# Seven normalised token tiles of the residual are copied by DMA into F32R tiles and transposed as F32R, and so is branch B's value tile, in a feed-forward and attention layer

## The chip, the cores and the metric

One core of one Trainium2 chip runs the whole kernel. The metric is the device time of one launch in microseconds, the median of repeated runs. A run here scatters by some tenths of a microsecond, and a difference of 0.2% is 3.8 us.

## What is computed

One layer over 1024 tokens of width 1024, all in float32:

```python
h = x + 0.5 * swiglu(rms_norm(x, ffn1_norm), ffn1_w_gate, ffn1_w_up, ffn1_w_down)   # D_FF = 2816
u = rms_norm(h, mix_norm)
qa, ka, va, qb, kb, vb, ga, gb = split(u @ w_in)                                    # 4352 columns
ya = neighbourhood_attention_2d(qa, ka, va, na_rpb)
yb = windowed_gqa_sink(rope(qb), rope(kb), vb, sink_logit)
h = h + (sigmoid(ga) * (ya @ w_branch_a) + sigmoid(gb) * (yb @ w_branch_b)) @ w_out
h = h + 0.5 * swiglu(rms_norm(h, ffn2_norm), ffn2_w_gate, ffn2_w_up, ffn2_w_down)
y = rms_norm(h, final_norm)
```

## The kernel before

The stages follow each other: the first feed-forward block, the projection to the 4352 columns, the two attentions with the merge, the second feed-forward block, and the last norm. Every large product is done by Strassen's seven products of half-size blocks, and every factor is split into a high part rounded to F32R (the reduced float32 type of TensorE) and the rest, so `mm3` issues three F32R matmuls of 128x512 for each block: high by high on L149, high by low on L153, low by high on L155. ACT makes the high part (L95, or L327 for weights) and DVE the low part (L98, L334). A tile named `g` or `d` is a PSUM bank, four of each; `fa` and `fx` are the residual and work rows, `ar` the right operands, `ws` the split left operands, `raw` and `ahead` loaded weights, `xs` two buffers of 128x1024.

Between a product that leaves the residual h in token rows and a product that needs the normalised rows turned (features on partitions) stands a `transition` (L167). There are two: the first between the down product of the first block and the projection (L1261), the second between the product with `w_out` and the second feed-forward block (L1815). The change works in these two. Eight tiles of 128 tokens pass through, and for tile t the steps are:

- `pre(t)`: from tile 4 on the tail of the finishing product (matmuls of TensorE into `g` or `d`, and the addition into the residual by DVE on L640), and a write of the row to DRAM from the SP queue.
- `normed` (L119): ACT squares the row into an `xs` buffer and sums it into the small tile `st` (L127), POOL adds epsilon and takes the power -1/2 (L130, L131), DVE scales the row into the same `xs` buffer (L133).
- `turned` (L137): eight transposes of 128x128 by TensorE on L142, with the `xs` block as weights and `ident` as the moving operand, into two `d` banks.
- `to_strassen` (L198): the operands of the next product. For tiles 0 to 3 they are split by L95 and L98 and copied by L211 and L212; from tile 4 on the Strassen sums stand in between (DVE L216, L218, L221, L222, then L95 and L98), and in the first transition a copy of a half row (L225).
- `post(t-1)`: from tile 4 on ten steps of the next product's matmuls, which are to cover the steps of the next tile.

The program issues tile t+1's `normed` ahead of tile t's `turned`, so the two `xs` buffers alternate: one is normed while the other is transposed. The buffer for the square of tile t+2 comes free when TensorE has transposed tile t. In the second transition the two tiles 4 and 5 are computed further ahead (`ahead` 3).

The order on every engine is fixed when the program is built: a scheduler places the instructions from the program order and its own estimates of durations, and what is pinned (`pin`) keeps its place. At run time each engine takes its own list in order, and an instruction that waits holds all behind it. POOL's list holds the `st` operations, and also the issue of every DMA of `nc.gpsimd` (writes of `hid`, `z_d`, `zs_d`, `g_d`).

In the projection stage `turn_v` (L1158) transposes branch B's values: a row block `vr` in an `xs` buffer, loaded by a DMA of the SP queue, 8 transposes on L1163 into `g` banks, and a split.

Of the kernel before, what the change touches and what calls it, by code (L numbers as in the profile page):

```python
# [9 lines left out]

F32 = mybir.dt.float32
# [4 lines left out]
P = 128  # L16
# [15 lines left out]
def f32v(ap):  # L32
    return ap.bitcast(F32)
# [3 lines left out]
def trunk_kernel(ctx, tc, x, xt, n1, wg1, wu1, wd1, nm, win, rpb, sink, wa, wb, wout,  # L37
# [16 lines left out]
    def nm_(s):  # L54
        uid[0] += 1
        return f"{s}_{uid[0]}"

    ident = const.tile([P, P], F32, name="ident")
    make_identity(nc, ident)
    nhalf4 = const.tile([P, 4], F32, name="nhalf")  # L60
    nc.gpsimd.memset(nhalf4, -0.5)
    nhalf = nhalf4[:, 0:1]
# [23 lines left out]
    def xs4():  # L86
        return main.tile([P, 1024], F32, tag="xs", bufs=2, name=nm_("xs"))
# [32 lines left out]
    def normed(h, gb, xs=None, parts=1):  # L120

        xs = xs4() if xs is None else xs
        w = D // parts
        cols = [slice(i * w, (i + 1) * w) for i in range(parts)]
        st = const.tile([P, 4], F32, tag="st", bufs=4, name=nm_("st"))
        for i, c in enumerate(cols):
            nc.scalar.activation(xs[:, c], h[:, c], AF.Square, scale=D ** -0.5, accum_out=st[:, i:i + 1])  # L127
        if parts == 2:
            nc.gpsimd.tensor_tensor(st[:, 0:1], st[:, 0:1], st[:, 1:2], op=ALU.add)
        nc.gpsimd.tensor_scalar(st[:, 0:1], st[:, 0:1], EPS, None, op0=ALU.add)  # L130
        nc.gpsimd.tensor_tensor(st[:, 2:3], st[:, 0:1], nhalf, op=ALU.pow)  # L131
        for c in cols:
            nc.vector.scalar_tensor_tensor(out=xs[:, c], in0=h[:, c], scalar=st[:, 2:3], in1=gb[:, c],  # L133
                                           op0=ALU.mult, op1=ALU.mult)
        return xs

    def turned(xs):  # L137
        pts = []
        for half in range(2):
            pt = bank("d")  # L140
            for c in range(4):
                nc.tensor.transpose(pt[:, c * P:(c + 1) * P], xs[:, (half * 4 + c) * P:(half * 4 + c + 1) * P], ident)  # L142
            pts.append(pt.rearrange("p (c t) -> p c t", c=4))
        return pts

# [18 lines left out]

        return fx[t] if t < 4 else fa[:, (t - 4) * 1024:(t - 3) * 1024]

    def transition(pre, gain, turn_tile, post, halves=1, ahead=2):  # L167

        h, xs = {}, {}
        n = NTT // halves  # L170
        for base in range(0, NTT, n):
            for t in (base, base + 1):
                h[t] = pre(t)
            xs[base] = normed(h.pop(base), gain)
            yield
            for t in range(base, base + n):
                for k in range(t + 2, t + 1 + ahead) if base and t == base else (t + (ahead if base else 2),):
                    if k < base + n:
                        h[k] = pre(k)
                if t + 1 < base + n:  # L180
                    xs[t + 1] = normed(h.pop(t + 1), gain)
                turn_tile(t, xs.pop(t))
                if t:
                    post(t - 1)
                yield
        post(NTT - 1)
# [6 lines left out]

    kept = []

    def to_strassen(t, xs):

        pa, pb = turned(xs)  # L198
        tt = t % 4
        cols = slice(tt * P, (tt + 1) * P)  # L200

        def put(o, src, eng=None):
            h, l = rhs(o)
            split(h[:, :, cols], l[:, :, cols], src, eng)

        x11 = res(tt)[:, :512].rearrange("p (c t) -> p c t", c=4)
        x21 = res(tt)[:, 512:].rearrange("p (c t) -> p c t", c=4)
        if t < 4:
            put(B11, pa)
            put(B21, pb)  # L210
            nc.scalar.copy(x11, pa)  # L211
            nc.scalar.copy(x21, pb)  # L212
            return
        t1 = res(t)[:, :512].rearrange("p (c t) -> p c t", c=4)
        t2 = res(t)[:, 512:].rearrange("p (c t) -> p c t", c=4)
        nc.vector.tensor_tensor(t1, pa, x11, op=ALU.subtract)  # L216
        put(T1, t1)
        nc.vector.tensor_tensor(t2, pb, t1, op=ALU.subtract)  # L218
        put(T2, t2)
        put(B22, pb)  # L220
        nc.vector.tensor_tensor(x11, t2, x11, op=ALU.subtract)  # L221
        nc.vector.tensor_tensor(x21, x21, t2, op=ALU.subtract)  # L222
        if kept:
            x12 = xs[:, :512] if t == NTT - 1 else main.tile([P, 512], F32, tag="s1", bufs=1, name=nm_("s1"))
            nc.scalar.copy(x12.rearrange("p (c t) -> p c t", c=4), pa)  # L225
            nc.sync.dma_start(kept[0][t - 4], x12)

# [190 lines left out]
    def behind(prods, sooner=()):  # L418

        run, load_ahead = prods[2:4]  # L420

        def post(t):
            if t >= 3:
                drain(run, 10)
            for i, n in zip((1, 2), sooner or (3, 4)):
                if t == n:
                    load_ahead(i)

        return post
# [484 lines left out]
    def keep_busy(n):  # L914

        b = bank("g")
        for i in range(n):
            k = i % 4 * P
            nc.tensor.transpose(b[:, k:k + P], ident, ident)

    def first_stage():
        load, _, _, _, pieces, (multiply, finish), hand_over, load_early = hg
# [39 lines left out]
        def do(op, a):  # L962
# [19 lines left out]
            elif op == "spread":  # L982
                i = int(a[0])
                r[i] = bank("d" if i else "g")
                for k in range(4):
                    nc.tensor.transpose(r[i][:, k * P:(k + 1) * P], st[i][0][:, k:k + 1].to_broadcast([P, P]), ident)
            elif op == "stat":
                t = int(a[0])
                nc.scalar.activation(toks[:, t - 4], toks[:, t - 4], AF.Square, scale=D ** -0.5,
# [162 lines left out]

    def v_b():
        mix["vb"] = [new_fx(k, F32R).rearrange("p (t d) -> p t d", t=NTT) for k in (0, 1)]
        mix["vr"] = xs4()
        pin(nc.sync.dma_start(mix["vr"], z_d[17 * P:18 * P, :]))

    def turn_v():  # L1158
        r = mix["vr"]
        for n in range(2):  # L1160
            pt = bank("g")
            for i in range(4):
                nc.tensor.transpose(pt[:, i * P:(i + 1) * P], r[:, (4 * n + i) * P:(4 * n + i + 1) * P], ident)  # L1163
            pt = pt.rearrange("p (b s d) -> p b s d", s=2, d=HD)
            for s in range(2):
                v = mix["vb"][s][:, 4 * n:4 * n + 4, :]
                split(v[:, :, :HD], v[:, :, HD:], pt[:, :, s, :])
# [446 lines left out]
    def turn(un):  # L1614
        nk = un["nk"]
        un["p"] = [ws4()[:, :768].rearrange("p (k s t) -> p k s t", k=3, s=2) for _ in range(2)]
        for s in range(2):
            pt = bank("d")
            for i in range(nk):
                nc.tensor.transpose(pt[:, i * P:(i + 1) * P], un["pr"][s][:, i * P:(i + 1) * P], ident)  # L1620
            if len(un["v"]) == 2:
                dst = [un["p"][s][:, :nk, k, :] for k in range(2)]
            else:
                dst = [un["p"][k][:, :nk, s, :] for k in range(2)]
            split(dst[0], dst[1], pt[:, :nk * P].rearrange("p (k t) -> p k t", k=nk))
# [186 lines left out]
        nc.sync.dma_start(h_d[t * P:(t + 1) * P, :], res(t))  # L1812
        return res(t)

    merge.into(transition(down2, gain, to_strassen, behind(hg), 2, 3), hg)  # L1815
    strassen_rest()
    drain(hg[2])
    gain = load_gain(nf)
# [122 lines left out]
```

## Time and profile before

| what | value |
|---|---|
| time, median of 3 runs | 1912.09 us (1911.81 to 1912.38) |
| the profiled execution's own time | 1912.05 us |
| its span on the core | 1910.1 us |
| TensorE busy, share of the span | 1901.1 us, 100% |
| VectorE (DVE) busy | 1456.1 us, 76% |
| ScalarE (ACT) busy | 961.3 us, 50% |
| GpSimd (POOL) busy | 244.3 us, 13% |
| first transition, transposes of tiles 4, 5 and 6 | begin at 639.91, 651.02 and 656.02 us |
| second transition, transposes of tiles 0 to 7 | from 1253.15 to 1293.84 us |

The span is the time from the first to the last instruction of the profile; 1.95 us of the execution's time lie outside it. In a row of the time line the first number is the start and the second the duration, from the start of the span, and `x8` after the shapes says that eight like instructions are merged in one row. In brackets stands the idle time of the engine before it, and what ended it. A matmul's duration includes its way through the array, so two matmuls overlap: what one costs is the distance between two starts.

### The profile page before, as it was taken

What the parts mean: (1) busy time and instruction counts of PE and PEld (TensorE: products, weight loads), DVE (VectorE), ACT (ScalarE), POOL (GpSimd) and SP (SyncE); (2) the same over time, 40 slices, a digit from 0 to 9 for tenths busy, and PEclk for the clock granted to TensorE, in tenths of its full rate; (3) what the DMA queues carried; (4) which work ended last, traced back from release to release, by engine and by line L of the source; (5) the groups of instructions that cost most, each with busy time, mean ns of one, the idle gap of its engine ahead of it and who ended that gap; (6) DMA issues with size and microseconds to landing.
All of it is one profiled execution on the core that took longest, in us unless ns stands there. A gap on an engine that the chain in (4) does not pass through costs nothing.

```text
span 1910.1 us, 26150 instructions
## 1 busy us (share of the span) xinstructions
PE 1901.1 (100%) x9020; PEld 1595.1 (84%) x9020; DVE 1456.1 (76%) x2644; ACT 961.3 (50%) x1876; POOL 244.3 (13%) x453
## 2 busy tenths in 40 slices
PE   9999999999999999999999999999999999999998
PEld 8888888888888888898898888888888888888886
DVE  8988888868957788666888999789665566559664
ACT  7533545544446543444898885274333333344453
POOL 0011232210000112211112300010010001000011
PEclk9999999999999999999999999999999999999999
DMA  7256977887454367855647969653333323492341
GB/s 270 95 188 217 336 273 289 298 293 282 127 166 135 112 206 225 243 192 206 181 123 207 296 227 335 232 195 132 136 111 107 108 89 111 162 357 93 110 139 61
DMA packets 176963, 365.84 MB, mean 192 GB/s; under 512 B 17728, under 2 KB 75968, under 8 KB 176832
## 3 DMA queue, kind: packets, MB, share of 16 engines
q1 hardware_dynamic: 136784, 236.23, 37.6%
q0 software_dynamic: 39184, 126.90, 19.2%
q8 instruction: 71, 1.16, 0.3%
q10 hardware_dynamic: 864, 1.05, 0.2%
q14 instruction: 60, 0.49, 0.1%
HBM read 244.06 MB, written 121.83 MB: 192 GB/s over the span
## 4 chain that ended last, share of the span: by engine, by line
PE 96%; ACT 2%; DVE 1%; DMA 0%; issue 0%; SPq 0%; POOLq 0%; POOL 0%; DVEq 0%
PE g L149 18%; PE g L155 18%; PE g L153 18%; PE d L155 12%; PE d L149 12%; PE d L153 12%; PE d L1620 2%; PE g L1634 1%; PE d L1596 1%; PE d L1597 1%; PE g L1639 1%; PE d L142 1%; ACT fa L1604 0%; ACT ws L95 0%; DMA fx<-in_xt_dram 0%; DVE ws L98 0%
## 5 line engine op out<-in xcount | busy, mean ns | idle before, releaser
L149 PE MATMUL g<-ar,ws 128*128 128x512 f32 x1062 | 407.0, 393 | 0.2
L153 PE MATMUL g<-ar,ws 128*128 128x512 f32 x1062 | 403.8, 390 | 0.0
L155 PE MATMUL g<-ar,ws 128*128 128x512 f32 x1062 | 402.6, 390 | 0.0
L149 PE MATMUL d<-ar,ws 128*128 128x512 f32 x706 | 275.3, 390 | 0.0
L155 PE MATMUL d<-ar,ws 128*128 128x512 f32 x706 | 274.9, 389 | 0.1
L153 PE MATMUL d<-ar,ws 128*128 128x512 f32 x706 | 274.8, 389 | 0.0
L155 PEld LDWEIGHTS g<-ar,ws 128*128 128x128 f32 x1062 | 199.2, 188 | 41.8
L153 PEld LDWEIGHTS g<-ar,ws 128*128 128x128 f32 x1062 | 199.4, 188 | 40.7
L149 PEld LDWEIGHTS g<-ar,ws 128*128 128x128 f32 x1062 | 196.4, 188 | 37.1 <-ACT xs L1331 1.1
L334 DVE TENSOR_TENSOR ws<-raw,ws 128x512 fp32r<-128x512 f32 x216 | 147.6, 689 | 78.5 <-ACT ws L327 77.7
L327 ACT CAST ws<-raw 128x512 fp32r<-128x512 f32 x216 | 132.7, 620 | 143.1 <-PE g L155 61.2
L155 PEld LDWEIGHTS d<-ar,ws 128*128 128x128 f32 x706 | 132.5, 188 | 28.0 <-DVE ws L334 0.5
L153 PEld LDWEIGHTS d<-ar,ws 128*128 128x128 f32 x706 | 132.6, 188 | 27.7 <-DVE ar L1000 0.3
L149 PEld LDWEIGHTS d<-ar,ws 128*128 128x128 f32 x706 | 132.7, 188 | 27.1
L95 ACT CAST ws<-raw 128x512 fp32r<-128x512 f32 x88 | 54.9, 623 | 115.5 <-PE d L155 63.6
L98 DVE TENSOR_TENSOR ws<-raw,ws 128x512 fp32r<-128x512 f32 x88 | 60.5, 688 | 55.2 <-ACT ws L95 55.1
L95 ACT CAST ar<-raw 128x512 fp32r<-128x512 f32 (+1 forms) x80 | 52.1, 654 | 84.4 <-PE g L153 51.5
L446 POOL DMA_DIRECT2D hid<-fx x91 | 49.5, 544 | 343.2 <-DVE fx L506 221.6
L149 PE MATMUL g<-ws,ws 128*128 128x512 f32 x232 | 90.9, 392 | 0.0
L153 PE MATMUL g<-ws,ws 128*128 128x512 f32 x232 | 90.3, 389 | 0.0
L155 PE MATMUL g<-ws,ws 128*128 128x512 f32 x232 | 90.1, 390 | 0.0
L95 ACT CAST ws<-ar 128x512 fp32r<-128x512 f32 x104 | 64.3, 618 | 47.4 <-PE g L155 25.4
(382 smaller groups left out, 3878.7 us busy)
## 6 DMA issues: line engine op xcount, KB each, us to landing
raw<-hid SPq DMA_DIRECT2D x70, 512.0 KB
hid<-fx POOLq DMA_DIRECT2D x91, 256.0 KB, 2.9
ar<-in_ffn_w_down_dram SPq DMA_DIRECT2D x32, 512.0 KB
raw<-in_ffn_w_up_dram SPq DMA_DIRECT2D x31, 512.0 KB
wo_d<-made POOLq DMA_DIRECT2D x28, 512.0 KB, 4.6
raw<-in_ffn_w_gate_dram SPq DMA_DIRECT2D x27, 512.0 KB
hid<-fa POOLq DMA_DIRECT2D x51, 256.0 KB, 2.9
ar<-zs_d POOLq DMA_DIRECT2D x48, 256.0 KB, 9.3
```

What stands on the lines that cost most here:

```text
L95: hi = nc.scalar.copy(dst_hi, src)
L98: (eng or nc.vector).tensor_tensor(dst_lo, src, f32v(dst_hi), op=ALU.subtract)
L142: nc.tensor.transpose(pt[:, c * P:(c + 1) * P], xs[:, (half * 4 + c) * P:(half * 4 + c + 1) * P], ident)
L149: o = nc.tensor.matmul(b, lhs[0], r[0], start=first, stop=False, **kw)
L153: nc.tensor.matmul(b, lhs[0], r[1], start=False, stop=False, **kw)
L155: nc.tensor.matmul(b, lhs[1], r[0], start=False, stop=last, **kw)
L327: nc.scalar.copy(w[0][:, :512], a)
L334: nc.vector.tensor_tensor(w[0][:, 512:], a, f32v(w[0][:, :512]), op=ALU.subtract)
L446: nc.gpsimd.dma_start(hid[PRODUCTS.index(p), i], src)
L1596: nc.tensor.matmul(b[:, :nw], un["q"][s], un["kd"][s][:, k0 * P:k1 * P], start=True, stop=False)
L1597: nc.tensor.matmul(b[:, :nw], un["q"][s], un["kl"][s][:, k0 * P:k1 * P], start=False, stop=True)
L1620: nc.tensor.transpose(pt[:, i * P:(i + 1) * P], un["pr"][s][:, i * P:(i + 1) * P], ident)
```

## The change

The identity is built as an F32R tile, by the same two POOL operations as before, and every transpose that is left in F32 takes it through a float32 view. `transition` gets a list `moved` of tiles, 5, 6 and 7 in the first and 0, 5, 6 and 7 in the second. For these, `normed` writes y to an `xs` buffer as before; then a second `xs` buffer `moved`, declared F32R, is allocated, and a pinned DMA of POOL's queue copies y into it (512 KB from SBUF to SBUF, L177). The eight transposes read the copy as F32R. Branch B's `vr` is declared F32R, is filled by the same DMA as before, and its eight transposes run as F32R. So 56 + 8 = 64 transposes change type. Since both tiles are of the pool of two, the buffer for a moved tile's copy must come free before its DMA is issued, and y's buffer is in use until that DMA has landed.

```diff
-    ident = const.tile([P, P], F32, name="ident")
-    make_identity(nc, ident)
+    ident = const.tile([P, P], F32R, name="ident")
+    nc.gpsimd.memset(f32v(ident), 0.0)
+    nc.gpsimd.affine_select(out=ident, in_=f32v(ident), compare_op=ALU.not_equal, fill=1.0, base=0, pattern=[[-1, P]],
+                            channel_multiplier=1)
...
     def turned(xs):
-        pts = []
+        i, pts = f32v(ident) if xs.dtype == F32 else ident, []
         for half in range(2):
             pt = bank("d")
             for c in range(4):
-                nc.tensor.transpose(pt[:, c * P:(c + 1) * P], xs[:, (half * 4 + c) * P:(half * 4 + c + 1) * P], ident)
+                nc.tensor.transpose(pt[:, c * P:(c + 1) * P].bitcast(xs.dtype), xs[:, (half * 4 + c) * P:(half * 4 + c + 1) * P], i)
...
-    def transition(pre, gain, turn_tile, post, halves=1, ahead=2):
+    def transition(pre, gain, turn_tile, post, halves=1, ahead=2, moved=(5, 6, 7)):
 
         h, xs = {}, {}
         n = NTT // halves
+
+        def norm(t):
+            x = y = normed(h.pop(t), gain)
+            if t in moved:
+                x = main.tile([P, 1024], F32R, tag="xs", bufs=2, name=nm_("moved"))
+                pin(nc.gpsimd.dma_start(f32v(x), y))
+            xs[t] = x, y
...
-            xs[base] = normed(h.pop(base), gain)
+            norm(base)
...
-                    xs[t + 1] = normed(h.pop(t + 1), gain)
-                turn_tile(t, xs.pop(t))
+                    norm(t + 1)
+                turn_tile(t, *xs.pop(t))
...
-    def to_strassen(t, xs):
+    def to_strassen(t, xs, spare):
...
-            x12 = xs[:, :512] if t == NTT - 1 else main.tile([P, 512], F32, tag="s1", bufs=1, name=nm_("s1"))
+            x12 = spare[:, :512] if t == NTT - 1 else main.tile([P, 512], F32, tag="s1", bufs=1, name=nm_("s1"))
...
     def v_b():
         mix["vb"] = [new_fx(k, F32R).rearrange("p (t d) -> p t d", t=NTT) for k in (0, 1)]
-        mix["vr"] = xs4()
-        pin(nc.sync.dma_start(mix["vr"], z_d[17 * P:18 * P, :]))
+        mix["vr"] = main.tile([P, 1024], F32R, tag="xs", bufs=2, name=nm_("vr"))
+        pin(nc.sync.dma_start(f32v(mix["vr"]), z_d[17 * P:18 * P, :]))
...
-                nc.tensor.transpose(pt[:, i * P:(i + 1) * P], r[:, (4 * n + i) * P:(4 * n + i + 1) * P], ident)
+                nc.tensor.transpose(pt[:, i * P:(i + 1) * P].bitcast(F32R), r[:, (4 * n + i) * P:(4 * n + i + 1) * P], ident)
...
-    merge.into(transition(down2, gain, to_strassen, behind(hg), 2, 3), hg)
+    merge.into(transition(down2, gain, to_strassen, behind(hg), 2, 3, (0, 5, 6, 7)), hg)
```

Lines of the changed kernel stand one further down than before up to the transition (L128 is the square, L131 and L132 the `st` operations, L134 the scaling, L143 the transposes), and eight further behind it (L648 for L640, L1124 for L1116).

The order of instructions changes on several engines. On ACT in the first transition, these are the rows between tile 5's and tile 7's squares before; `xs_5391` is tile 6's buffer:

```order
L127 ACTIVATE xs_5310,st_5311<-fa 128x1024
L127 ACTIVATE xs_5391,st_5392<-fa 128x1024
L95 CAST ar_5219<-fa 128x4x128
L95 CAST ar_5218<-fa 128x4x128
L95 CAST ar_5220<-d_5321 128x4x128
L225 COPY s_609_5336<-d_5316 128x512
L327 CAST ws_5250<-raw_5228 128x512
L1116 ACTIVATE fa<-g_5339 128x512
L95 CAST ar_566<-fx_75 128x4x128
```

In the changed kernel the same place of ACT reads so; `xs_5393` is tile 6's buffer:

```order
L128 ACTIVATE xs_5310,st_5311<-fa 128x1024
L96 CAST ar_5219<-fa 128x4x128
L233 COPY s_610_5338<-d_5318 128x512
L96 CAST ar_5218<-fa 128x4x128
L96 CAST ar_5220<-d_5323 128x4x128
L96 CAST ar_566<-fx_75 128x4x128
L335 CAST ws_5250<-raw_5228 128x512
L1124 ACTIVATE fa<-g_5341 128x512
L128 ACTIVATE xs_5393,st_5394<-fa 128x1024
```

Tile 6's square stood ahead of the seven casts and copies that follow tile 4's transposes, and stands behind them now.

On DVE at the front of the second transition, before; `xs_11709`, `xs_11737` and `xs_11790` are tiles 0, 1 and 2, and `d_11743`, `d_11748` the banks of tile 0's transposes:

```order
L133 SCALAR_TENSOR_TENSOR xs_11709<-fx_11171,st_11710,gain_11308 128x1024
L98 TENSOR_TENSOR ws_11673<-ar_9785,ws_11673 128x512
L133 SCALAR_TENSOR_TENSOR xs_11737<-fx_11172,st_11738,gain_11308 128x1024
L98 TENSOR_TENSOR ws_11690<-ar_9785,ws_11690 128x512
L98 TENSOR_TENSOR ws_11715<-ar_9785,ws_11715 128x512
L98 TENSOR_TENSOR ar_11732<-d_11743,ar_11732 128x4x128
L98 TENSOR_TENSOR ar_11733<-d_11748,ar_11733 128x4x128
```

And in the changed kernel, with `xs_11745` for tile 1:

```order
L134 SCALAR_TENSOR_TENSOR xs_11715<-fx_11177,st_11716,gain_11314 128x1024
L99 TENSOR_TENSOR ws_11679<-ar_9791,ws_11679 128x512
L99 TENSOR_TENSOR ws_11696<-ar_9791,ws_11696 128x512
L99 TENSOR_TENSOR ws_11723<-ar_9791,ws_11723 128x512
L134 SCALAR_TENSOR_TENSOR xs_11745<-fx_11178,st_11746,gain_11314 128x1024
L99 TENSOR_TENSOR ar_11740<-d_11751,ar_11740 128x4x128
L99 TENSOR_TENSOR ar_11741<-d_11756,ar_11741 128x4x128
```

Tile 1's scaling moved behind two weight splits, and still stands ahead of the low parts of tile 0; four L640 and tile 2's scaling follow in both.

On POOL in the second transition, from tile 5's `st` operations (`st_11919`) to tile 7's (`st_12057`), before:

```order
L130 TENSOR_SCALAR st_11919<-st_11919 128x1
L131 TENSOR_TENSOR st_11919<-st_11919,nhalf 128x1
L130 TENSOR_SCALAR st_11984<-st_11984 128x1
L131 TENSOR_TENSOR st_11984<-st_11984,nhalf 128x1
L130 TENSOR_SCALAR st_12057<-st_12057 128x1
L131 TENSOR_TENSOR st_12057<-st_12057,nhalf 128x1
```

And in the changed kernel:

```order
L131 TENSOR_SCALAR st_11927<-st_11927 128x1
L132 TENSOR_TENSOR st_11927<-st_11927,nhalf 128x1
L177 DMA moved_11932<-xs_11926 128x1024
L131 TENSOR_SCALAR st_11994<-st_11994 128x1
L132 TENSOR_TENSOR st_11994<-st_11994,nhalf 128x1
L177 DMA moved_11999<-xs_11993 128x1024
L131 TENSOR_SCALAR st_12069<-st_12069 128x1
L132 TENSOR_TENSOR st_12069<-st_12069,nhalf 128x1
L177 DMA moved_12074<-xs_12068 128x1024
```

Each copy stands ahead of the next tile's `st` operations. On TensorE, 30 matmuls stood between tile 5's and tile 6's transposes of the second transition, and 18 stand there now; the twelve others stand behind tile 6's. In the first transition 18 stand there in both kernels; between tile 6's transposes and the next matmul into a `g` bank four matmuls into `d` stood before, and six stand there now.

More of the change, by code (lines that the diff above doesn't have):

```diff
@@ L7 @@
 from concourse import mybir
-from concourse.masks import make_identity
 from concourse._compat import with_exitstack
@@ L918, in keep_busy @@
             k = i % 4 * P
-            nc.tensor.transpose(b[:, k:k + P], ident, ident)
+            nc.tensor.transpose(b[:, k:k + P], f32v(ident), f32v(ident))
     def first_stage():
@@ L985, in do @@
                 for k in range(4):
-                    nc.tensor.transpose(r[i][:, k * P:(k + 1) * P], st[i][0][:, k:k + 1].to_broadcast([P, P]), ident)
+                    nc.tensor.transpose(r[i][:, k * P:(k + 1) * P], st[i][0][:, k:k + 1].to_broadcast([P, P]), f32v(ident))
             elif op == "stat":
@@ L1619, in turn @@
             for i in range(nk):
-                nc.tensor.transpose(pt[:, i * P:(i + 1) * P], un["pr"][s][:, i * P:(i + 1) * P], ident)
+                nc.tensor.transpose(pt[:, i * P:(i + 1) * P], un["pr"][s][:, i * P:(i + 1) * P], f32v(ident))
             if len(un["v"]) == 2:
```

## The prediction

> **What bounds the kernel now.** I read the page first: the busy times, the clock and the shares of the chain that ended last.
>
> ```profile
> span 1910.1 us, 26150 instructions
> PE 1901.1 (100%) x9020; PEld 1595.1 (84%) x9020; DVE 1456.1 (76%) x2644; ACT 961.3 (50%) x1876; POOL 244.3 (13%) x453
> PEclk9999999999999999999999999999999999999999
> PE 96%; ACT 2%; DVE 1%; DMA 0%; issue 0%; SPq 0%; POOLq 0%; POOL 0%; DVEq 0%
> ```
>
> TensorE is busy for 1901.1 of 1910.1 us at full clock, and 96% of the chain is its own. So it has no slack that another engine's gain could use: whatever TensorE no longer does comes off the time, and whatever it newly waits comes on. The question is only how much shorter 64 transposes become, and where a copy of some microseconds, which now stands between normalisation and transposes, arrives late.
>
> Next the groups by line, kept apart by shape, for the transposes and the weight loads (mean ns of one before the last bar), and the time line of TensorE around one group of eight and around matmuls of 512 and 256 columns:
>
> ```profile
> L142 PE MATMUL d<-ident,xs 128*128 128x128 f32 x128 | 16.6, 272 | 0.0
> L142 PEld LDWEIGHTS d<-ident,xs 128*128 128x128 f32 x128 | 14.7, 140 | 2.4 <-issue 0.5 <-ACT fx L212 0.2
> L153 PEld LDWEIGHTS g<-ar,ws 128*128 128x128 f32 x1062 | 199.4, 188 | 40.7
> ```
>
> ```profile
> 584.64 0.39 PE L155 MATMUL g<-ws,ws 128*128 128x512 f32 x1
> 584.86 1.03 PE L142 MATMUL d<-ident,xs 128*128 128x128 f32 x8
> 585.65 0.47 PE L149 MATMUL g<-ws,ws 128*128 128x512 f32 x1
> 585.97 0.39 PE L153 MATMUL g<-ws,ws 128*128 128x512 f32 x1
> ...
> 641.25 0.40 PE L155 MATMUL g<-ar,ws 128*128 128x512 f32 x1
> 650.79 0.40 PE L155 MATMUL g<-ar 128*128 128x512 f32 x1
> ...
> 810.74 0.28 PE L153 MATMUL d<-ws,ar 128*128 128x256 f32 x1
> 810.86 0.28 PE L155 MATMUL d<-ws,ar 128*128 128x256 f32 x1
> ```
>
> From start to start a 128x512 F32R matmul takes 0.227 us (42 of them lie between 641.25 and 650.79), a 128x256 one 0.12. Eight F32 transposes and the matmul behind them take 585.97 - 584.86 = 1.11 us; less that matmul's 0.227 the group costs 0.88, or 0.110 each. That is nearly what 256 columns of F32R cost, for 128 columns.
>
> **The gain.** No F32R instruction with 128 columns stands in the trace, so I bound it. The columns alone: (0.227 - 0.120) / 256 x 128 = 0.0535 us each. The straight line through both sizes, its constant included: 0.120 - 0.0535 = 0.066. The other end is 0.110, no gain at all: each transpose loads its own weights, and an F32R weight load lasts 188 ns against 140 for these F32 loads, so the load could set the pace. But F32R loads of 188 ns follow each other every 0.12 us in the 256-column rows without holding the matmuls up, so I take 0.060, in the middle of the first two. A moved tile saves 8 x 0.050 = 0.40 us, and so does `turn_v`: 8 groups, **-3.2 us** (0 to 8 x 8 x 0.0565 = -3.6).
>
> The Trainium skill, "TensorE: Matmul & The Clock Gate", Part 1, under "Wait — 56ns, not 53.3ns?", states 55.6 ns from start to start for back-to-back matmuls of 128 columns, measured in another type; by that the gain would be 64 x 0.054 = 3.5 us, and the sum below would end 0.3 us lower.
>
> **The first transition, where tile 6 waits.** The rows of DVE, of ACT and of TensorE; the first number is the start, the brackets hold the idle time before:
>
> ```profile
> 640.37 1.28 DVE L133 SCALAR_TENSOR_TENSOR xs<-fa,st,gain 128x1024 f32<-128x1024 f32 x1 [2.24 <-POOL st L131]
> 642.17 0.68 DVE L216 TENSOR_TENSOR fa<-d,fx 128x512 f32<-128x512 f32 x1
> 647.29 1.28 DVE L133 SCALAR_TENSOR_TENSOR xs<-fa,st,gain 128x1024 f32<-128x1024 f32 x1
> 657.15 1.28 DVE L1120 SCALAR_TENSOR_TENSOR fa<-g,fa 128x512 f32<-128x512 f32 x2
> ```
>
> ```profile
> 638.22 1.06 ACT L127 ACTIVATE xs<-fa 128x1024 f32<-128x1024 f32 x1 [2.98 <-DVE fa L640]
> 643.42 1.12 ACT L95 CAST ar<-fa 128x512 fp32r<-128x512 f32 x2
> 646.42 0.62 ACT L95 CAST ar<-fx 128x512 fp32r<-128x512 f32 x1
> ```
>
> ```profile
> 651.02 1.04 PE L142 MATMUL d<-ident,xs 128*128 128x128 f32 x8
> 657.89 0.50 PE L149 MATMUL g<-ar,ws 128*128 128x512 f32 x1
> ```
>
> From the start of a square to the start of its scaling pass 640.37 - 638.22 = 2.15 us, two POOL operations among them. Tile 6's square needs the buffer of tile 5's y, which the copy reads, and stands behind the seven casts and copies of tile 4. Those took 643.42 to 647.04 before; without tile 6's square ahead of them they can begin when L216 ends, at 642.85, and end near 646.5. The copy of tile 5 is issued when y is ready at 641.65 and, by the rows of DMA below, lands at 645.2 to 646.3, so ACT's queue and not the copy decides. The scaling starts at 646.5 + 2.15 = 648.65, 1.36 us later than the 647.29 of before. Behind it DVE has no break worth the name until L1120, which frees the `g` bank for the matmul at 657.89. Its first half ended at 657.15 + 0.68 = 657.83; now it ends at about 659.2. TensorE alone would come to that matmul at 657.89 - 0.80 (two faster groups) + 0.45 (two more `d` matmuls ahead of it) = 657.54. Wait: **+1.7 us**, 0 if ACT's and DVE's small breaks swallow the delay, 2.5 if the casts come later still. Tile 6's own copy cannot begin until tile 5's transposes free a buffer, at 651.6, and lands at 655.1 to 656.2, where its transposes are due at 656.02 - 0.40 = 655.6: covered within half a microsecond that the other wait contains.
>
> The nearest rows for a copy, 512 KB on POOL's queue, are of other places (KB each, median us from issue to landing):
>
> ```profile
> ar<-wo_d POOLq DMA_DIRECT2D x8, 512.0 KB, 3.5
> wo_d<-made POOLq DMA_DIRECT2D x28, 512.0 KB, 4.6
> zr_d<-xs POOLq DMA_DIRECT2D x5, 512.0 KB, 6.7
> ```
>
> I take 3.5 us where the DMA engines are mostly idle and 4.6 where they are busy.
>
> **The second transition, where the front waits.** Here the rows of DVE and of TensorE, and two stretches with the busy time of the engines, and at the end the clock, the DMA share and GB/s:
>
> ```profile
> 1246.66 1.28 DVE L133 SCALAR_TENSOR_TENSOR xs<-fx,st,gain 128x1024 f32<-128x1024 f32 x1 [0.45 <-POOL st L131]
> 1254.41 1.29 DVE L98 TENSOR_TENSOR ar<-d,ar 128x512 fp32r<-128x512 f32 x2 [2.43 <-ACT ar L95]
> 1255.61 2.48 DVE L640 SCALAR_TENSOR_TENSOR fa<-g,fa 128x512 f32<-128x512 f32 x4
> 1258.00 1.28 DVE L133 SCALAR_TENSOR_TENSOR xs<-fx,st,gain 128x1024 f32<-128x1024 f32 x1
> ```
>
> ```profile
> 1253.15 1.03 PE L142 MATMUL d<-ident,xs 128*128 128x128 f32 x8
> 1259.49 1.03 PE L142 MATMUL d<-ident,xs 128*128 128x128 f32 x8
> ```
>
> ```profile
> 1240.00:1250.00 10.00, 10.00 (x46) 8.28 (x45) 6.65 (x9) 4.10 (x8) 3.43 (x5) 1.00 0.77 260
> 1250.00:1260.00 10.00, 10.00 (x56) 8.43 (x55) 7.19 (x12) 5.83 (x11) 1.10 (x4) 1.00 0.61 220
> ```
>
> Tile 0's y is ready at 1247.94; with 4.6 us (shares 0.77 and 0.61) its copy lands at 1252.5, before its transposes at 1253.15. But tile 1's square now needs y's buffer: 1252.5 + 2.15 puts its scaling at 1254.7, and it stands ahead of tile 0's low parts, which began at 1254.41. They begin at 1255.9, and two L98, four L640 and tile 2's scaling follow without a break: 1255.9 + 1.2 + 2.4 + 1.28 = 1260.8. Tile 2's transposes at 1259.49, less the 0.40 of tile 0, were due at 1259.1: **+1.7 us**, 0.6 with a copy of 3.5, 2.8 with one of 5.7.
>
> **The second transition, where tile 6 waits.** Again DVE's scaling of tile 6, TensorE's transposes of tiles 4 and 5, and two stretches:
>
> ```profile
> 1274.07 1.27 DVE L133 SCALAR_TENSOR_TENSOR xs<-fa,st,gain 128x1024 f32<-128x1024 f32 x1
> ```
>
> ```profile
> 1270.37 1.04 PE L142 MATMUL d<-ident,xs 128*128 128x128 f32 x8
> 1278.09 1.03 PE L142 MATMUL d<-ident,xs 128*128 128x128 f32 x8
> ```
>
> ```profile
> 1270.00:1280.00 10.00, 10.00 (x54) 8.45 (x53) 10.00 (x16) 6.59 (x13) 0.87 (x2) 1.00 0.89 303
> 1280.00:1290.00 10.00, 10.00 (x50) 8.37 (x49) 10.00 (x17) 9.73 (x18) 1.43 (x3) 1.00 0.20 60
> ```
>
> Tile 5's copy is issued when tile 4's transposes free a buffer, at 1271.4, and lands with 4.6 us (share 0.89) at 1276.0, 2.1 ahead of its transposes. Tile 6's square can start only then, some 0.6 later behind a cast, so its scaling moves from 1274.07 to 1278.75 and ends at 1280.0; tile 6's copy (share 0.20, 3.5 us) lands at 1283.5. The order has 18 matmuls left between the two groups of transposes: due at 1278.09 + 8 x 0.060 + 18 x 0.227 = 1282.65. **+0.9 us**, 0 to 2.2 (both copies at 4.6). Tile 7 has 39 matmuls, 8.9 us, ahead of it, which cover its copy.
>
> **At nothing:** `turn_v`'s load stays on SP's queue, so only its transposes change; the identity's two POOL operations stay, at the start. On POOL the next tile's `st` pair and some `z_d` or `hid` writes stand behind a waiting copy; the pairs are late only as the squares are, which is in the sum, and the writes are read a stage later. Cover gone, each write would come later by a copy's wait, some 1 to 4 us, with nobody due.
>
> **Sum:** -3.2 + 1.7 + 1.7 + 0.9 = +1.1. Against the profiled execution's 1912.05 (span 1910.1 and 1.95 outside it; 0.04 under the median of 1912.09) that is **1913.2 us**.
>
> **The rivals.** *Slow copies* (chance 0.13, the slower side). All seven copies take 6.7 us, as `zr_d<-xs` does. The shares 0.77 and 0.89 speak for it in the second transition, the 3.5 and 4.6 of two rows of the same size against it. Then the first transition's tile 6 lands 2.7 late; at the front tile 0 itself is late and tile 2 with it, 3.8 in all; at tile 6 two copies stand in series, 2 x 6.7 - 7.8 = 5.6 late. -3.2 + 12.1 gives 1921.0. With a landing L the three waits are 1.7 + (L - 2.9) + (2L - 7.8); they pass 7.06, the point of "slower", from L = 5.4 on. The Trainium skill, "DMA: Bandwidth & Descriptors", section "Issuing engines are not separate DMA queues", says that DMAs of all issuing engines end on the same 16 engines and interleave: it speaks against this change where weights are loaded, as in the stretch with share 0.89.
>
> *Transposes no faster* (0.12). The weight load sets the pace, and 0.110 stays. Then the waits shrink too, since TensorE comes later by 0.40 a group: 0.9 + 1.3 + 0.5, so 1914.8.
>
> *All waits hidden* (0.17). Copies land quickly, the casts on ACT run ahead, and DVE's breaks take the rest: -3.2 alone, 1908.9. Against it stands DVE, which is busy all 10.00 us of both last stretches.
>
> **How the numbers follow.** A measurement here can tell about 0.2%, 3.8 us, from no change: 1908.27 to 1915.91. My case has 0.53, and 0.05 is left for gains that I don't see, as from matmuls that the order now places better. Even the whole gain of 3.6 us stays within the bound, so faster has only those 0.05. Slower has the slow copies' 0.13 and 0.02 from the top of my own case. Its own bounds, waits of 0.6 us with the gain of 3.6 and waits of 7.5 with that of 3.2, give 1909.1 to 1916.4; the range reaches down to the hidden waits: 1908.8 to 1916.4, with the slow copies and a little more outside.
>
> **What would show it.** In the profile after, eight groups of transposes from start to the next matmul but one 0.40 shorter; a wait of TensorE near 657.5 for DVE's L1120 (a `g` bank), one at tile 2 of the second transition for the scaling L134, one at tile 6 of it for a DMA into `moved`; copies of 3.5 to 4.6 us. If TensorE shows no idle time there, the waits were hidden and the gain was all; if groups last 0.88 as before, the gain was none; if copies take over 5.4 us, slower.

## The result: 9 us slower, and the profile after

The changed kernel takes 1921.76 us in the median of 6 runs (1919.01 to 1924.02), the kernel before 1912.50 beside it (1911.81 to 1913.25). The ratio is 1.0048, 95% interval 1.0036 to 1.0061: slower, above the range of the prediction. The profiled execution took 1920.52 us with a span of 1918.7; the numbers below account for its 8.6 us over the span of before.

The page of the changed kernel first, and then who TensorE waited for in it (us in total, times, longest). Before, that view had one row, the 1.5 for the identity at the start.

```profile
span 1918.7 us, 26176 instructions
PE 1902.2 (99%) x9020; PEld 1593.4 (83%) x9020; DVE 1456.4 (76%) x2644; ACT 962.0 (50%) x1876; POOL 247.9 (13%) x460
```

```profile
PE d L143 <- DMA moved<-xs: 2.2, 2, 1.7
PE d L1604 <- DVE nmx L1609: 1.7, 1, 1.7
PE g L927 <- POOL ident L59: 1.5, 1, 1.5
PE g L150 <- ACT fx L220: 0.7, 1, 0.7
PE d L143 <- DVE xs L134: 0.7, 1, 0.7
PE d L150 <- ACT ar L1006: 0.6, 1, 0.6
...
PE g L150 <- DVE fa L648: 0.4, 1, 0.4
PE d L150 <- ACT ws L335: 0.3, 1, 0.3
PE g L150 <- DVE fa L1128: 0.2, 1, 0.2
```

TensorE has idle time now, and PE's busy time is even a microsecond longer. The transposes did get shorter. Here is tile 5's group in the first transition:

```profile
651.63 0.80 PE L143 MATMUL d<-ident,moved 128*128 128x128 f32 x8
652.26 0.47 PE L150 MATMUL g<-ar,ws 128*128 128x512 f32 x1
652.57 0.40 PE L154 MATMUL g<-ar,ws 128*128 128x512 f32 x1
```

By the reckoning of the prediction, 652.57 - 651.63 - 0.227 = 0.71 us against 0.88: a group gains 0.17 us, not 0.40, and eight groups 1.3 us.

The front of the second transition on TensorE, and then tile 6:

```profile
1255.76 0.39 PE L156 MATMUL g<-ar 128*128 128x512 f32 x1
1256.66 0.84 PE L143 MATMUL d<-ident,moved 128*128 128x128 f32 x8 [0.52 <-DMA moved<-xs]
...
1260.20 1.04 PE L143 MATMUL d<-ident,xs 128*128 128x128 f32 x8
1261.96 0.48 PE L150 MATMUL g<-ws,ws 128*128 128x512 f32 x1 [0.72 <-ACT fx L220]
...
1263.89 0.39 PE L156 MATMUL g<-ws,ws 128*128 128x512 f32 x1
1264.99 1.06 PE L143 MATMUL d<-ident,xs 128*128 128x128 f32 x8 [0.71 <-DVE xs L134]
```

```profile
1288.02 0.39 PE L156 MATMUL g<-ar,ws 128*128 128x512 f32 x1
1290.12 0.84 PE L143 MATMUL d<-ident,moved 128*128 128x128 f32 x8 [1.72 <-DMA moved<-xs]
...
1291.10 0.40 PE L154 MATMUL d<-ar,ws 128*128 128x512 f32 x1
1291.78 0.80 PE L150 MATMUL d<-ar,ws 128*128 128x512 f32 x1 [0.28 <-ACT ws L335]
1292.38 0.63 PE L154 MATMUL d<-ar,ws 128*128 128x512 f32 x1
...
1294.94 0.50 PE L156 MATMUL g<-ar,ws 128*128 128x512 f32 x1
```

The idle time in brackets is short of the loss by some 0.16 us, since a 512-column matmul's duration of 0.39 outlasts its distance of 0.227. Counted from start to start the losses are 0.67 at tile 0, 0.97 at the `g` bank behind tile 1's transposes (1.76 instead of 0.79), 0.87 at tile 2, 1.87 at tile 6, and 0.45 and 0.37 behind it. Then something happens that no wait shows: from 1292.38 to 1294.94 six matmuls stand, 0.427 us apart instead of 0.227. That is 1.20 us more. The windows (the last three columns are granted clock, DMA share, GB/s) say what it is:

```profile
1290.00:1292.00 2.00, 1.59 (x11) 1.19 (x12) 2.00 (x4) 1.93 (x4) 0.60 (x2) 0.94 0.00 0
1292.00:1294.00 2.00, 2.00 (x5) 1.61 (x6) 1.50 (x2) 1.97 (x3) 0.65 (x1) 0.50 0.00 0
1294.00:1297.00 3.00, 3.00 (x12) 2.38 (x11) 2.49 (x4) 0.29 (x2) 1.17 (x2) 0.81 0.64 179
```

What is missing to a clock of 1.00 makes (0.06 x 2 + 0.50 x 2 + 0.19 x 3) / 0.50 = 3.4 us at 0.50, from 1291.75 on, behind the largest wait. The matmul of 1291.78 stands in it too, so about 0.2 of the 0.37 is the clock's as well. The Trainium skill, "TensorE: Matmul & The Clock Gate", Part 1, section "HAM oscillation — how this bites in real kernels", has the rule: a wait long enough puts the array back to half its clock. It puts the limit at idle gaps of about 3.4 us; here a wait of 1.87 us and the first part of the short one behind it did it (the last section has the rows).

The chain behind these waits, first on DVE, then on POOL and ACT:

```profile
1249.50 1.28 DVE L134 SCALAR_TENSOR_TENSOR xs<-fx,st,gain 128x1024 f32<-128x1024 f32 x1 [0.46 <-POOL st L132]
...
1258.78 1.28 DVE L134 SCALAR_TENSOR_TENSOR xs<-fx,st,gain 128x1024 f32<-128x1024 f32 x1 [3.96 <-POOL st L132]
...
1261.18 2.48 DVE L648 SCALAR_TENSOR_TENSOR fa<-g,fa 128x512 f32<-128x512 f32 x4
1263.57 1.27 DVE L134 SCALAR_TENSOR_TENSOR xs<-fx,st,gain 128x1024 f32<-128x1024 f32 x1
...
1284.33 1.28 DVE L134 SCALAR_TENSOR_TENSOR xs<-fa,st,gain 128x1024 f32<-128x1024 f32 x1 [0.77 <-POOL st L132]
```

```profile
1251.09 0.62 POOL L177 DMA_DIRECT2D moved<-xs  x1 [1.62 <-DVE xs L134]
1277.02 0.62 POOL L177 DMA_DIRECT2D moved<-xs  x1 [3.03 <-PE d L143]
1286.16 0.61 POOL L177 DMA_DIRECT2D moved<-xs  x1 [1.86 <-PE g L156]
```

```profile
1256.61 1.06 ACT L128 ACTIVATE xs<-fx 128x1024 f32<-128x1024 f32 x1 [2.52 <-DMA moved<-xs]
...
1281.81 1.07 ACT L128 ACTIVATE xs<-fa 128x1024 f32<-128x1024 f32 x1
...
1290.07 1.06 ACT L128 ACTIVATE xs<-fa 128x1024 f32<-128x1024 f32 x1 [0.80 <-DMA moved<-xs]
```

Tile 0's y is ready at 1249.50 + 1.28 = 1250.78; its copy is issued at 1251.09 and has landed when tile 1's square starts at 1256.61: 5.8 us where the sum had 4.6. Tile 1's scaling then comes at 1258.78, the four L648 from 1261.18 on, and the end of the first of them, 1261.86, frees the `g` bank for the matmul at 1261.96. (The row names ACT's L220, which ends at 1261.88 and reads a `d` bank. The reader of the `g` bank is L648, and the program makes the matmul wait for the bank; the trace cannot tell the two apart.) At tile 6, y is ready at 1285.61, and its copy lands when tile 7's square starts at 1290.07: 4.5 us where the sum had 3.5, and tile 5's took 4.8 from its issue.

The span's sum, by place: second transition 0.67 + 0.97 + 0.87 + 1.87 + 0.45 + 0.37 + 1.20 = 6.4; first transition 0.9 (the rows for L648 and L1128, from start to start); a wait in attention A, 1.9 (the row for L1609); 0.6 more at the start, which is scatter (see the first experiment); gain -1.3. That is 8.5 of the 8.6.

### The profile page after: what moved, and what is told of

Same layout as the page of the kernel before. It is cut to its first block, busy times and chain, and to the rows that moved or that the text cites. A ratio compares the mean times of both kernels' runs of the same rounds, so it can differ in the third digit from the quotient of the medians.

```text
span 1918.7 us, 26176 instructions
## 1 busy us (share of the span) xinstructions
PE 1902.2 (99%) x9020; PEld 1593.4 (83%) x9020; DVE 1456.4 (76%) x2644; ACT 962.0 (50%) x1876; POOL 247.9 (13%) x460
```

## Experiments

**The changed kernel again**, without an edit, for a second profile. 

> The changed kernel once more, for a second profile. Theory (the copies make TensorE wait in both transitions, and the largest wait, ahead of tile 6 of the second transition, lets the clock fall for some microseconds): the same waits at tiles 0, 2 and 6 of the second transition come back, and 512-column matmuls at 0.43 instead of 0.227 us from start to start behind tile 6 again; about 1921 us. Rival (the waits at the start, 0.6 us, and in attention A, 1.9 us, belong to the change too): these two come back as well.

1919.26 us (1916.82 to 1924.05, 7 runs; before 1912.74), profile 1919.14. The waits of the second transition came back, 1.28 at tile 0, 0.90, 0.89, 1.66 at tile 6, and six matmuls at half clock behind it. The 1.9 of attention A did not. So the first set was there in both profiles of the change, and that wait in one. The wait at the start came back too, with 0.8. The row that shows it (L982, the matmuls with `ones`) starts at 14.07 and 14.35 us in these two profiles, at 13.52 before, and anywhere from 13.12 to 14.06 in those of the kernels below, with and without copies, so I count it as scatter.

**Branch B's values alone.** Both `moved` lists are empty:

```diff
-    down.into(transition(down1, gain, to_strassen, behind(pg, (0, 1)), 2), pg)
+    down.into(transition(down1, gain, to_strassen, behind(pg, (0, 1)), 2, moved=()), pg)
...
-    merge.into(transition(down2, gain, to_strassen, behind(hg), 2, 3, (0, 5, 6, 7)), hg)
+    merge.into(transition(down2, gain, to_strassen, behind(hg), 2, 3, ()), hg)
```

> Only the value tile of branch B stays F32R, no copies at all in the transitions. Theory: one group of eight gains what the trace of the changed kernel shows, 0.88 - 0.72 = 0.17 us, so 1912.3, not to be told from before. By the prediction's step of 0.40 it would be 1912.1. Rival (the identity as F32R or the changed order at the start costs something): over 1913.

1912.59 (10 runs) beside 1912.74; ratio 1.0000 (0.9990 to 1.0009). The identity and the start cost nothing that can be told.

**The copies without F32R transposes.**

```diff
-                x = main.tile([P, 1024], F32R, tag="xs", bufs=2, name=nm_("moved"))
-                pin(nc.gpsimd.dma_start(f32v(x), y))
+                x = main.tile([P, 1024], F32, tag="xs", bufs=2, name=nm_("moved"))
+                pin(nc.gpsimd.dma_start(x, y))
```

> The seven copies stay, but into F32 tiles, and the transposes of the seven tiles run as F32; the value tile stays F32R. Theory (seven groups of F32R gain 7 x 0.165 = 1.2 us and the copies cost some 10): the copies' cost stays, with TensorE coming a little later to each wait, so 1921 to 1923, above or like the changed kernel. Rival (the F32R transposes themselves disturb TensorE, its clock or its order): near before, 1912 to 1914.

1922.42 (1918.90 to 1925.57, 5 runs); ratio 1.0045 (1.0030 to 1.0060). The whole loss is there with F32 transposes, so the copies make it, with the order of instructions that comes with them.

**The F32R transposes without copies.** Here y is rounded to F32R as DVE writes it, so the operands lose their low parts:

```diff
-            x = y = normed(h.pop(t), gain)
-            if t in moved:
-                x = main.tile([P, 1024], F32R, tag="xs", bufs=2, name=nm_("moved"))
-                pin(nc.gpsimd.dma_start(f32v(x), y))
+            x = y = normed(h.pop(t), gain, main.tile([P, 1024], F32R, tag="xs", bufs=2, name=nm_("xs")) if t in moved else None)
...
-            x12 = spare[:, :512] if t == NTT - 1 else main.tile([P, 512], F32, tag="s1", bufs=1, name=nm_("s1"))
+            x12 = xs4()[:, :512] if t == NTT - 1 else main.tile([P, 512], F32, tag="s1", bufs=1, name=nm_("s1"))
```

> No copies: DVE and ACT write the seven normalised tiles straight into F32R tiles, which are transposed as F32R; so y is rounded to F32R before the split, and the half row of the last tile goes to a buffer of its own. Theory: 64 transposes at the pace the trace shows gain 8 x 0.165 = 1.3 us, 1911.2. By the prediction's 0.060 us a transpose: 3.2, 1909.3. Rival (F32R transposes bring waits of their own): 1912 or over.

1910.93 (10 runs) beside 1912.74; ratio 0.9991 (0.9982 to 1.0000). Once more with five rounds:

> The seven tiles written as F32R by DVE and ACT (y rounded), no copies, once more with five rounds. Theory: 0.165 us for each of eight groups, 1.3 us under before. By the prediction's step: 3.2 under before.

1910.88 (1910.48 to 1911.45, 11 runs) beside 1912.70; ratio 0.9986 (0.9977 to 0.9995). That is 1.8 us less: nearer to 1.3 than to 3.2. The lowest runs lie 1.3 and 1.2 us apart (1910.58 against 1911.87, 1910.48 against 1911.68), and four of the 15 runs of the kernel before stand over 1915 here, so the median of before may hold part of the 1.8. It is the only version here that beats both kernels, and it pays with the rounding. In its trace a group costs 0.70 to 0.72 us again.

**One transition or tile at a time**, by the `moved` lists alone: the first transition; the second; tile 0 of the second; tiles 5, 6, 7 of the second.

> Copies and F32R only in the first transition (tiles 5, 6, 7) and for branch B's values; the second transition as before. Theory (the loss is made where TensorE waits): 4 groups gain 0.7 us, the waits at the first transition are 1.0, so +0.3, 1913.0; with the attention wait of 1.9 us, if it hangs on these copies, 1914.9. Rival (all copies cost alike, 10 us over seven): +4, 1916.5.

> Copies and F32R only in the second transition (tiles 0, 5, 6, 7) and for the values; the first as before. Theory: 5 groups gain 0.8 us; waits of 0.7 to 1.3 at tile 0, 0.9 at tile 1's matmul, 0.9 at tile 2, 1.7 at tile 6, 0.8 behind it and some 1.5 for the lower clock make 6.6, so +5.8, 1918.4, with the scatter of the changed kernel. Rival (seven copies cost alike): +5.5 as well, told from the first by its profile alone.

> Of all copies only that of tile 0 of the second transition, and the values. Theory: three waits of 0.7 to 1.3, 0.9 and 0.9 us at tiles 0, 1 and 2 against a gain of 0.3: +2.4, 1915.0. The prediction's step had 1.7 against 0.8: 1913.5.

> Only tiles 5, 6, 7 of the second transition, and the values. Theory: the waits at tile 6 and behind it (1.7 + 0.8) and the lower clock (1.5) against a gain of 0.7: +3.3, 1916, with a clock of 0.5 in a stretch of 2 us behind tile 6 in the profile. The prediction's step had 0.9 against 1.6: 1912.

| copies | median (range), 10 runs each | over before (1912.65) | ratio (95% interval) |
|---|---|---|---|
| first transition | 1916.06 (1912.99 to 1919.88) | 3.4 | 1.0013 (1.0001 to 1.0024) |
| second transition | 1918.76 (1915.85 to 1921.01) | 6.1 | 1.0027 (1.0017 to 1.0036) |
| tile 0 of the second | 1915.39 (1913.91 to 1917.29) | 2.7 | 1.0010 (1.0001 to 1.0020) |
| tiles 5, 6, 7 of the second | 1916.94 (1915.21 to 1921.94) | 4.3 | 1.0019 (1.0010 to 1.0029) |

The ratios put each loss 0.7 to 0.9 us lower than the medians do. The second transition came out as expected, within 1 us in both parts. The profile with tile 0 alone has the longest landing of all. Here is TensorE's wait for it, and the copy's time from its issue:

```profile
PE d L143 <- DMA moved<-xs: 1.5, 1, 1.5
```

```profile
DMA to landing us min/median/max: 6.5/6.5/6.5
```

With tiles 5, 6, 7 alone, tile 6's transposes start at 1284.88 after 2.42 us of idle time, and the clock is at half from there on. (The row names DVE's L230; tile 6's copy lands at that moment too, since tile 7's square, which waits for it, starts at 1284.82.)

```profile
1282.07 0.39 PE L156 MATMUL g<-ar,ws 128*128 128x512 f32 x1
1284.88 1.23 PE L143 MATMUL d<-ident,moved 128*128 128x128 f32 x8 [2.42 <-DVE fx L230]
...
1286.88 0.63 PE L150 MATMUL d<-ar,ws 128*128 128x512 f32 x1
1287.31 0.63 PE L154 MATMUL d<-ar,ws 128*128 128x512 f32 x1
```

The first transition did not. Its median lies near the rival's 1916.5, but no run does: its ten runs lie in two heaps, five from 1913.0 to 1914.4 and five from 1917.7 to 1919.9, and its profile fell into the lower one, with the 1.0 us of waits that the theory had and, but for the start, nothing else.

**The same kernel twice more, for an upper run seen from inside.**

> The kernel with the first transition's copies alone, once more, for its profile. Theory: a run of 1916 or over shows DVE waiting 2 us or more in attention A for a write of y, or the clock at half behind such a wait; a run near 1913 shows neither. Rival: an upper run has its loss in the transition itself.

> The same once more, since a single run falls into the lower runs in some three of ten. Theory and rival as in the run before this one.

The first took 1918.07, the second 1914.47. In the first one, TensorE and DVE in attention A, 440 us behind the copies, and the windows there:

```profile
1103.55 0.46 PE L1604 MATMUL d<-ar 128*128 128x384 f32 x1 [4.14 <-DVE nmx L1609]
...
1104.55 0.63 PE L154 MATMUL g<-ar,ws 128*128 128x512 f32 x1
1104.98 0.63 PE L156 MATMUL g<-ar,ws 128*128 128x512 f32 x1
```

```profile
1102.60 0.42 DVE L1572 TENSOR_TENSOR fa<-g,s 64x256 f32<-64x256 f32 x1 [4.49 <-DMA y_d<-fa]
```

```profile
1100.00:1102.00 2.00, 0.00 (x0) 0.00 (x0) 0.00 (x0) 0.00 (x0) 0.57 (x2) 1.00 1.17 222
...
1104.00:1106.00 2.00, 2.00 (x8) 1.61 (x7) 2.00 (x7) 1.11 (x4) 0.00 (x0) 0.50 1.01 337
```

DVE may not overwrite `fa` until a write of y to DRAM has landed; the 16 DMA engines are full there (1.17), and DVE stands 4.5 us for it. TensorE idles 4.1 us, and then the clock is at 0.50. The second run has the same wait with 1.3 us and no fall of the clock, the run before none. So the one upper run that was seen from inside is this wait, with the clock behind it; that the others are is likely. What it has to do with copies 440 us earlier is the question of the next runs.

**Copies that nobody reads**, in two halves to tiles of the `hs` pool, while the transposes are F32 and take y itself. First in the first transition, then with 128x8 elements each, then in the second transition alone:

```diff
-                x = main.tile([P, 1024], F32R, tag="xs", bufs=2, name=nm_("moved"))
-                pin(nc.gpsimd.dma_start(f32v(x), y))
+                z = [main.tile([P, 512], F32R, tag="hs", bufs=6, name=nm_("moved")) for _ in range(2)]
+                for k in range(2):
+                    pin(nc.gpsimd.dma_start(f32v(z[k]), y[:, k * 512:(k + 1) * 512]))
```

> The first transition's three copies go to tiles that nobody reads, and its transposes are F32 as before; no copies in the second; the values F32R. It tells what makes the upper runs of the run with the first transition alone (1917.7 to 1919.9 beside 1913.0 to 1914.4). Theory (three more transfers on POOL's queue shift what it issues later, and attention's saturated DMA engines then make DVE wait): the upper runs stay, some of ten at 1916 or over. Rival (the waits in the transition themselves lower the clock in some runs): all runs near 1912.4.

> As the unread copies in the first transition (six transfers of 256 KB on POOL's queue), but each of 128x8 elements, 4 KB. Theory (the number of transfers, or the order around them, shifts what attention's loads collide with): upper runs stay, some of ten over 1914. Rival (the bytes): all runs at 1912 to 1913, like before.

> The second transition's four copies go to tiles that nobody reads (eight transfers of 256 KB), its transposes are F32 as before; the first transition as before, the values F32R. Theory (the copies cost by standing between the scaling and the transposes, and by holding y's buffer): y's buffer is still held until its copy has landed, but the transposes take y itself and the next square takes the other buffer, so no wait at tiles 0, 1 and 6: 1912.3 to 1913. Rival (the transfers themselves crowd out the weight loads of that stage): 1914 or over.

| unread copies | median (range), 11 runs each | runs over 1914 |
|---|---|---|
| first transition | 1914.17 (1911.83 to 1920.67) | 7 |
| first, 128x8 each | 1913.12 (1912.23 to 1916.62) | 4 |
| second transition | 1913.13 (1912.41 to 1917.68) | 3 |

The kernel before had 3 of 21 runs over 1914 beside the last two (1911.59 to 1916.98), and 2 of 21 beside the first (up to 1920.05). Over all sets here 17 of its some 115 runs lie over 1914, so upper runs are more frequent with the copies and not new; none of those 17 was seen from inside. The upper runs of the first row stay without any wait in the transition, and its profile shows 2.7 us of TensorE waiting for L1610's `nmx` in attention A. So the rival (the waits there lower the clock in some runs) falls. The middle row lies between; that the bytes and not the number of transfers count is likely, but 4 and 7 of 11 don't show it. The last row settles the second transition: with the same transfers at the same place, and nobody behind them, the median is 0.6 us over before (ratio 1.0005, 0.9996 to 1.0014), not 6.1. DVE's list at the front has its old order again in this run, so it takes away the reader and the new order together. The rows of the changed kernel tell these apart: the last of the weight splits that moved ahead of tile 1's scaling there ended at 1254.81, and DVE then stood idle for 3.96 us, until the landed copy had let tile 1's square and its `st` pair through.

**The first transition's copies issued by SP**, `nc.sync.dma_start` in place of `nc.gpsimd.dma_start`, the second transition as before:

> As the run with the first transition alone, but SP's queue issues the three copies, so POOL's queue has as many transfers as before. Theory (POOL's queue shifted): no upper runs, about 1913 in all. Rival (waits of the transition): upper runs stay. The copies may start later or earlier behind SP's loads; 1912.5 to 1914 in the lower runs either way.

1920.80 (1918.30 to 1924.09, 5 runs). In its profile a copy makes tile 6's transposes wait 1.0 us, and attention A's wait is there with 2.4 and half clock behind it. POOL's queue is not what shifts; my theory of it falls.

**A buffer of their own for the copies**, two `hs` tiles each, read by the transposes:

> All seven copies, each into two 128x512 F32R tiles of a pool of its own (two transfers of 256 KB) in place of the second xs buffer; same F32R transposes. Theory (the copy costs by holding the next tile's square off the xs buffers): the waits at the g bank and tile 2 of the front and at tile 6 go, with the fall of the clock; tile 0's own landing stays at 0.7 to 1.7 us; gain 1.3; 1912 to 1913, or some 4 more where attention waits as in the first-transition run. Rival (the transfer itself is too slow for its place, whoever owns the buffers): tile 6 and tile 0 wait as before, 1917 or over.

1926.53 (1920.96 to 1929.14, 4 runs): the worst of all, and against my theory. ACT, DVE and TensorE at tile 6 of its second transition:

```profile
1280.78 1.06 ACT L128 ACTIVATE xs<-fa 128x1024 f32<-128x1024 f32 x1 [3.98 <-DMA moved<-xs]
```

```profile
1282.47 0.69 DVE L99 TENSOR_TENSOR ar<-fa,ar 128x512 fp32r<-128x512 f32 x1 [1.89 <-ACT ar L96]
```

```profile
1290.52 0.47 PE L151 MATMUL d<-ar,ws 128*128 128x512 f32 x1 [1.36 <-DVE ar L99]
```

With buffers of their own the scheduler places tile 7's square earlier on ACT, and it still needs the `xs` buffer of tile 5's y, which the copy holds until it lands. Now the casts of the operands queue behind it. The copy's time has only moved to another list. The profile is of the fastest of the four runs, so what adds 5.6 us more in their median was not seen.

**All sixteen tiles as F32R without copies**, `moved` full in both:

> All sixteen tiles and the values F32R without copies, y rounded to F32R by DVE as it is written. Theory (0.165 us a group): 17 groups gain 2.8, 1909.9. By the prediction's 0.40 a group: 6.8, 1905.9. If the 1.8 us of eight groups measured before scale: 3.8, 1908.9.

1914.12 (1913.62 to 1916.37, 11 runs) beside 1912.37; ratio 1.0011 (1.0002 to 1.0019): slower, none of the three numbers. In its profile (the slowest of its runs, 1916.37, with attention's wait of 2.0) TensorE waits 0.9 us for a scaling L134 in the first transition and 0.8 for L645, DVE's addition into the residual. That earlier and reordered transposes meet DVE there is argued, not shown.

## Why the prediction was wrong

- **The bound** was right: TensorE had no slack, and each wait of it came onto the time.
- **The transposes.** "I take 0.060, in the middle of the first two" failed. A group went from 0.88 to 0.71, 0.089 us per transpose with its share of the change of type, and -3.2 was -1.3 (1.8 in the runs without copies). In an unhindered group only the first two distances are short (0.058 and 0.069 us), the other six are 0.081 to 0.090. The 256-column rows could not exclude a pace set by the weight loads below 0.12; I let them decide against the rival that had it. That the loads set this pace was not tried; they last 140 ns here, as for F32, and not the 188 that the prediction took. The 55.6 ns that the prediction cites from the Trainium skill ("TensorE: Matmul & The Clock Gate", Part 1, "Wait — 56ns, not 53.3ns?") were measured in another type; by them the gain would have been 3.5, and only the first two distances here come near them.
- **The copies' price.** "3.5 us where the DMA engines are mostly idle and 4.6 where they are busy" failed by about a microsecond each: from y's end to its landing 5.8 at the front and 4.5 at tile 6, and 6.5 from the issue in the run with tile 0 alone. The rows of other transfers count from the issue; 0.3 to 0.5 us of issuing come on top.
- **The front's chain** was right, and so was its formula. L - 2.9 gives 2.9 with L = 5.8; 0.67 + 0.97 + 0.87 = 2.5 were measured. I had named tile 2 alone; tile 0 itself waited as well, and so did the `g` bank that L648 frees, ahead of tile 2.
- **Tile 6** was right in place and in form: the term had 0.9 and 1.87 were measured. The steps of the term make 2L - 7.2, not the 2L - 7.8 of the rival, which leaves out the 0.6 behind a cast; with the landings of 4.8 and 4.5 that is 2.1. The 0.45 for a weight split that comes late behind it was missed.
- **The first transition**: 0.9 for 1.7, in two places. Tile 6's scaling came as reckoned (649.23, which is 648.65 and the 0.6 of the start). But two groups of transposes gained 0.17 each and not 0.40, so TensorE came to the bank some 0.5 later and waited less.
- **What the sum had no term for**: the clock, at least 1.20 us behind tile 6, and attention A, 1.9 us in this profile and up to 4.1. Both turn a wait, or a margin, into more than its length.
- **The rivals.** "Slow copies" gave 1921.0, nearly the number that came, with copies of 6.7 us. But the copies took 3.0 to 5.4 us from their issue in this profile, 4.4 in the median, and the missing microseconds were the clock and attention A. So its number is right for only half its reason, and the rest of it is luck.

## What to carry to other kernels

Price an instruction that you have never seen at its new size from both sides, and take the unfavourable side where another unit (here the weight loads) might set the pace. Between a producer and TensorE a copy costs its landing from the producer's end, and it holds the source buffer as well: look for the instruction that waits for that buffer, and what queues behind it. On a TensorE without slack a wait of about 2 us is not only its length: look behind it for matmuls at half clock.

## What the hardware showed that I had not expected

- The granted clock fell to 0.50 behind 1.4 to 2.4 us of idle time at or behind tile 6 in five of the copying profiles, and behind 2.4 and 4.1 us in attention A in two. Each of the seven falls lasted 3.41 us. A wait of 1.7 us in the run with F32 copies and one of 2.7 in attention A with unread copies had no fall behind them. So the length alone does not decide it. What fits is where a wait lies: in each trace the rises and falls of the clock are whole multiples of 3.413 us apart, and if the trace is cut into stretches at these points, TensorE was idle for 1.57 to 3.13 us of the stretch ahead of each fall, and, up to the end of the program, for at most 1.66 us of any other. (The two overlap by 0.1, so this share may not be the whole rule.) In the first two rows, of the changed kernel, one wait fills most of a stretch; in the last two the 2.7 us with unread copies are split over two stretches (the second number is TensorE's busy time, the third from the end the clock):

```profile
1288.33:1291.75 3.42, 1.45 (x11) 0.97 (x10) 3.42 (x7) 2.53 (x6) 0.35 (x2) 1.00 0.09 37
1291.75:1295.16 3.41, 3.38 (x8) 2.71 (x9) 2.68 (x4) 2.42 (x3) 1.52 (x2) 0.50 0.05 11
...
1096.72:1100.13 3.41, 2.19 (x17) 1.74 (x15) 0.89 (x3) 1.46 (x4) 1.41 (x3) 1.00 1.23 258
1100.13:1103.55 3.42, 1.90 (x12) 1.72 (x13) 2.84 (x10) 1.81 (x5) 0.63 (x2) 1.00 1.03 299
```

- F32R transposes of 128 columns settle at some 0.085 us, between the F32 ones (0.109) and half of them.
- The write of y in attention A lands with a margin that the profile of before keeps and some of the other profiles do not. Transfers early in the kernel made runs over 1914 more frequent (7 of 11 with unread copies, 2 of 21 beside them); why they reach so far is left open.
